# The low halves of pieces read back from device memory: a VectorE subtract in place of a ScalarE copy and an accumulating transfer

## The chip, the cores and the metric

One core of one Trainium2 chip runs the whole kernel. The metric is the device time of the kernel in microseconds; lower is better. Engines are named as the profile names them: PE is TensorE, PEld its weight loads, DVE is VectorE, ACT is ScalarE, POOL is GpSimd, SP is SyncE, which here issues nearly all DMAs.

## What is computed

One step of a hybrid encoder layer over 2048 prompt frames and 8 x 16 sample frames, 1024 channels, all in float32. The projection makes eight blocks of 1024 columns; branch a mixes positions and goes through `w_o_a`, branch b is a gated convolution of 31 taps with a layer norm and `w_o_b`; both are gated, added and go through `w_out`.

```python
h = _rmsnorm(x, norm_g) * (1 + scale) + shift
z = h @ w_in + b_in
u, v, gate_a, glu_a, glu_b, gate_b, merge_a, merge_b = jnp.split(z, SPLITS, axis=-1)
y_a = jax.nn.gelu(u) * _spatial_proj(_layernorm(jax.nn.gelu(v), ln_v_g, ln_v_b), w_spatial, b_spatial)
y_a = (y_a * jax.nn.silu(gate_a)) @ w_o_a
g_cat = jnp.concatenate([conv_hist, glu_a * jax.nn.sigmoid(glu_b)], axis=1)
dw = lax.conv_general_dilated(g_cat, conv_w[:, None, :], (1,), 'VALID', ...) + conv_b
y_b = (jax.nn.silu(_layernorm(dw, ln_c_g, ln_c_b)) * jax.nn.silu(gate_b)) @ w_o_b
m = jax.nn.sigmoid(merge_a) * y_a + jax.nn.sigmoid(merge_b) * y_b
x = x + gate * (m @ w_out)
```

## The kernel before

**Products in halves.** Matmuls take operands rounded to a shorter format (fp32r in the profile). To keep float32's digits, every operand is split in two: hi is the rounded value, lo the rest, and a product is three matmuls, hi with hi, hi with lo, lo with hi. Names end in h and l (ya4h, ya4l; wh, wl). `split` is the usual way to make the two: ScalarE copies hi (L592), VectorE subtracts lo = value - hi (L594).

**Groups and stages.** The rows are worked on in three groups of 768, 768 and 640 columns (channels lie on the 128 partitions, rows of the sequence along the columns). The stages follow each other as first_products(0), branch_a(0), first_products(1), branch_a(1), branch_b(0), first_products(2), branch_a(2), output(0), branch_b(1), branch_b(2); `prepare` makes the next group's normed input between them. What doesn't fit into on-chip memory between stages is put away: `put` (L709) stores a tile of 128 rows in device memory, under names such as away_ya, away_ma, away_dw, away_sum, and `get` (L714) reads it back into a slot (yab, mab, dwb, sumb). All such tiles lie in one pool of 47 slots, tag "u"; a tile that takes over a slot waits until the old one's readers are done, stores among them.

**What reads pieces back in halves.** `halves_of` does it for the eight tiles ya of each branch_a, and for the eight tiles ma of output(0): 32 calls. It gets the tile, copies hi on ScalarE (L722), copies lo = -hi on ScalarE (L724), and then `added` (L700) lets a DMA on GpSimd's queue add the tile from device memory onto lo. branch_a multiplies ya with `w_o_a` (`product`, L615, tiles oa) and the result with the sigmoid of merge_a (L1180, mab, put away as ma).

**First products in seven.** first_products makes a pair of column blocks with seven products instead of eight (Strassen's scheme, `strassen`, L660; ga, gb, ma, mb and so on are its outputs, bga, bgb, bma, bmb its bank B in PSUM, acga, acgb its banks A and C). On bank B products A11, S2, S3 and A22 are added up one after another; between two of them `snap` (L671, ScalarE) copies the bank out as it stands, so the next of them waits for that copy. VectorE adds bank C (L681) and banks A and C (L685). The last column blocks of a group (mb, gb) stand in TensorE's order beside the first products of branch_a.

**The convolution** is 31 taps per tile on VectorE (L951, tile dw, reading the tile gb or gsb that comes back from away_g; its first tap is ScalarE's, L936). The layer norm's statistics in branch_b start from sumb (dmh L592, dml L594) and end in sums over partitions (dv, L529).

**What sets the order.** No order is written out. `Plan` gathers all operations with a cost in us, a due time and, for transfers, a lag, and simulates five engines: an engine takes, of its operations that are ready and have a slot, the one that is due first. In that order the instructions are issued, each engine in sequence. So an operation that is added, taken away or moved to another engine changes the order of others too.

Of the kernel before, what the change touches and what calls it, by code (L numbers as in the profile page):

```python
# [9 lines left out]
F32 = mybir.dt.float32  # L10
F32R = mybir.dt.float32r
AF = mybir.ActivationFunctionType
# [72 lines left out]
class Plan:  # L85
# [22 lines left out]
    def op(self, eng, cost, fn, reads=(), writes=(), due=0.0, nb=-1, step=None, func=None,  # L108
           commute=False, lat=0.0):
        o = Op()  # L110
        o.eng, o.cost, o.fn, o.due, o.nb, o.step, o.func = eng, cost, fn, due, nb, step, func
        o.lat = lat
        o.users, o.ready, o.seq = [], 0.0, len(self.ops)
        deps = set()
        vals = set()
        for x in reads:
            p = x if isinstance(x, Part) else x.part(None)
            vals.add(p.val)
            deps.update(p.writers)
            p.readers.append(o)  # L120
        for x in writes:
            p = x if isinstance(x, Part) else x.part(None)
            vals.add(p.val)
            if commute and p.commuting and not p.readers:
                p.writers.append(o)
                continue
            deps.update(p.readers)
            deps.update(p.writers)
            p.writers, p.readers, p.commuting = [o], [], commute
        deps.discard(o)  # L130
        for d in deps:
            d.users.append(o)
        o.n_deps = len(deps)
        o.vals = list(vals)
        for v in vals:
            v.uses += 1
        self.ops.append(o)
        return o
# [102 lines left out]
def c_dve(n):  # L241
    return n / 960.0 + 0.13
# [6 lines left out]
def c_act(n, fixed=0.15):  # L249
    return n / 1200.0 + fixed  # L250
# [7 lines left out]
def encoder_kernel(ctx: ExitStack, tc: tile.TileContext, xT, hist0, cT, w_ada, w_cols, w_v,  # L258
                   vecs, convw, wsT, bsp, bv_row, lnv_rows,
                   yT, ncp, ncs, vout):  # L260
    nc = tc.nc
# [11 lines left out]
    op = plan.op  # L273
# [25 lines left out]
    def slot(name, dt=F32):  # L299
        uid[0] += 1  # L300
        return plan.val("u", [P, UW], dt, f"{name}_{uid[0]}")
# [47 lines left out]
    def new_step():  # L349
# [7 lines left out]
       reads=[vec], writes=[vec], due=-9)  # L357
    op("pool", 0.5, lambda: make_identity(nc, ident.t), writes=[ident])
    op("dve", 0.1, lambda: nc.vector.tensor_tensor(fold.t, ident.t[:, :9], ident.t[:, 9:18], op=ALU.add),
       reads=[ident], writes=[fold], due=-9)  # L360
    op("pool", 0.3, lambda: nc.gpsimd.memset(ones.t, 1.0), writes=[ones])
    op("act", 0.3, lambda: nc.scalar.activation(ones_r.t, ones.t, AF.Copy), reads=[ones], writes=[ones_r],
       due=-6)
    op("pool", 0.2, lambda: nc.gpsimd.memset(half.t, -0.5), writes=[half])
    op("act", 0.3, lambda: nc.scalar.activation(cin.t, cin.t, AF.Silu), reads=[cin], writes=[cin],
       due=-9, func="silu")
# [223 lines left out]
    def split(src, n, due, name):  # L590
        hi, lo = slot(f"{name}h", F32R), slot(f"{name}l", F32R)
        op("act", c_act(n, 0.1), lambda: nc.scalar.activation(hi.t[:, :n], src.t[:, :n], AF.Copy),  # L592
           reads=[src], writes=[hi], due=due)
        op("dve", c_dve(n), lambda: nc.vector.tensor_tensor(  # L594
            lo.t[:, :n], src.t[:, :n], hi.t[:, :n].bitcast(F32), op=ALU.subtract),
           reads=[src, hi], writes=[lo], due=due)
        return hi, lo
# [100 lines left out]
    def added(out, out_ap, src, src_ap, due):  # L698

        op("pool", C_ADD, lambda: nc.gpsimd.dma_start(out=out_ap(), in_=src_ap(), accum_op=ALU.add),  # L700
           reads=src, writes=out, due=due, lat=L_ADD)


    away = {}
# [7 lines left out]
    def get(x, j, n, due, nb):  # L712
        a, v = away[x, j], slot(f"{x[0]}b")
        op("sp", n * 512 / 340e3, lambda: nc.sync.dma_start(out=v.t[:, :n], in_=a.t[:, :n]),  # L714
           reads=[a], writes=[v], due=due, nb=nb, lat=3.5)
        return v

    def halves_of(x, j, n, due):

        v, a = get(x, j, n, due - 1, due - 2), away[x, j]  # L720
        hi, lo = slot(f"{x[0]}{j}h", F32R), slot(f"{x[0]}{j}l", F32R)
        op("act", c_act(n, 0.1), lambda: nc.scalar.activation(hi.t[:, :n], v.t[:, :n], AF.Copy),  # L722
           reads=[v], writes=[hi], due=due)
        op("act", c_act(n, 0.1), lambda: nc.scalar.activation(  # L724
            lo.t[:, :n], hi.t[:, :n].bitcast(F32), AF.Copy, scale=-1.0), reads=[hi], writes=[lo], due=due + 0.01)
        added([lo], lambda: lo.t[:, :n].bitcast(F32), [a], lambda: a.t[:, :n], due + 0.02)
        return hi, lo


    def segments(gi, b0, bn):  # L730
# [437 lines left out]
    def branch_a(gi):  # L1168

        ns, npr, p0 = GROUPS[gi]  # L1170
        n = ns + npr
        nt, nh = n // P, n // 2
        last = gi == len(GROUPS) - 1
        cuts = halves(n)
        sA = step_no[0]
        ya = [halves_of(("ya", gi), k, n, sA - 2 + k * 0.1) for k in range(KC)]
        for j in range(KC):
            ps, st = product(W_OA + j, ya, wide(n), f"oa{gi}_{j}")
            m = get(("ma", gi), j, n, st, st - 1)
            op("dve", c_dve(n), lambda m=m, b=(lambda ps=ps, m=m: banks(ps, m, n)): nc.vector.tensor_tensor(  # L1180
                b()[1], b()[0], b()[1], op=ALU.mult), reads=[ps, m],
               writes=[m], due=st + 1.5)
            put(("ma", gi), j, m, n, st + 1.6)
# [63 lines left out]
    def output(gi, ms=None):  # L1247
# [6 lines left out]
        if ms is None:  # L1254
            ms = [halves_of(("ma", gi), k, n, step_no[0] - 2 + k * 0.1) for k in range(KC)]
# [51 lines left out]
    for q in range(4):  # L1307
        due, scale_whole, shift_whole = ADA[q]
        ada("scale", q, 4 * q * D, due, scale_whole)
        ada("shift", q, (4 * q + 2) * D, due, shift_whole)  # L1310
    h = prepare(0, due=0, nb=-1, dr=DR)
# [6 lines left out]
    h = prepare(1, due=step_no[0] + PREP_DUE, nb=step_no[0] + PREP_NB)  # L1318
# [3 lines left out]
    h = prepare(2, due=step_no[0] + PREP_DUE, nb=step_no[0] + PREP_NB)  # L1322
# [67 lines left out]
```

## Time and profile before

| | us |
|---|---|
| median of 3 runs (lowest to highest) | 2112.56 (2109.44 to 2116.53) |
| profiled execution: its own time | 2110.4 |
| its span, first to last instruction | 2108.7 |
| TensorE busy | 2060.6 (98%) |
| VectorE busy | 1693.0 (80%) |
| ScalarE busy | 931.0 (44%) |
| GpSimd busy | 89.5 (4%) |

The mean granted TensorE clock over the span is 0.992 of full speed. Busy time counts instructions that run, not issue or waiting.

### The profile page before, as it was taken

The numbers are of one execution on the slowest core, as the hardware profiler recorded it, in microseconds if no ns is written. First come the engines' busy times: TensorE is split into PE (matmuls) and PEld (weight loads), VectorE is DVE, ScalarE is ACT, GpSimd is POOL, SyncE is SP. The second block draws the span as 40 slices with busy tenths as digits, with TensorE's granted clock in tenths as the row PEclk, the third lists the DMA queues.
The fourth block names the chain that finished last, engine by engine and source line by source line (L and its number), as shares of the span: only waits on it lengthen the run. The fifth ranks groups of instructions, "written<-read, shape, count | busy, mean of one in ns | idle before, by whom it ended". The sixth has DMA issues, their size and how long they took to land.

```text
span 2108.7 us, 33303 instructions
## 1 busy us (share of the span) xinstructions
PE 2060.6 (98%) x12810; PEld 1966.2 (93%) x12810; DVE 1693.0 (80%) x2407; ACT 931.0 (44%) x1356; POOL 89.5 (4%) x107
## 2 busy tenths in 40 slices
PE   7999999999999999999999999999999999999997
PEld 3999998999979999999998889999999999888997
DVE  5759988999899969688547899769999974956855
ACT  3354455455642343444446432434544544523432
POOL 0000000000100000000001010000000011010000
PEclk9999999999999999999999999999999999999998
DMA  8538777688975477887889876599989999376463
GB/s 328 205 141 295 260 298 270 225 312 294 318 252 204 137 264 247 279 262 246 285 262 324 312 218 181 174 342 335 335 300 319 335 314 342 119 232 221 154 196 118
DMA packets 190927, 540.58 MB, mean 256 GB/s; under 512 B 22064, under 2 KB 39728, under 8 KB 190768
## 3 DMA queue, kind: packets, MB, share of 16 engines
q1 hardware_dynamic: 180256, 511.11, 68.3%
q0 software_dynamic: 10512, 27.33, 7.4%
q8 instruction: 101, 1.65, 0.3%
q14 instruction: 58, 0.48, 0.1%
HBM read 375.47 MB, written 162.89 MB: 255 GB/s over the span
## 4 chain that ended last, share of the span: by engine, by line
PE 87%; DMA 6%; DVE 3%; issue 2%; ACT 0%; SPq 0%; POOL 0%; POOLq 0%; DVEq 0%; ACTq 0%
PE v L1032 9%; PE ob L615 9%; PE out L615 7%; PE bga L660 5%; PE bgla L660 5%; PE bu L660 5%; PE oa L615 4%; PE bglb L660 4%; PE bma L660 4%; PE bmb L660 4%; PE acga L660 3%; PE acu L660 3%; PE acgla L660 3%; PE acma L660 3%; PE bgb L660 3%; PE acglb L660 3%
## 5 line engine op out<-in xcount | busy, mean ns | idle before, releaser
L951 DVE SCALAR_TENSOR_TENSOR dw<-gb,cw,dw 128x768 f32<-128x768 f32 (+1 forms) x720 | 658.5, 924 | 37.8 <-ACT dw L936 32.2
L384 DVE TENSOR_TENSOR w<-ra,w 128x1024 fp32r<-128x1024 f32 x112 | 121.6, 1087 | 37.3 <-ACT w L382 36.3
L382 ACT ACTIVATE wh<-wr 128x1024 fp32r<-128x1024 f32 x88 | 91.9, 1053 | 133.7 <-PE ob L615 76.5
L382 ACT ACTIVATE w<-ra 128x1024 fp32r<-128x1024 f32 x112 | 105.6, 947 | 61.6 <-PE acgla L660 17.4
L384 DVE TENSOR_TENSOR wl<-wr,wh 128x1024 fp32r<-128x1024 f32 x88 | 106.9, 1216 | 3.3 <-ACT wh L382 3.3
L384 DVE TENSOR_TENSOR w<-rb,w 128x512 fp32r<-128x512 f32 x112 | 75.4, 685 | 40.6 <-ACT w L382 40.4
L382 ACT ACTIVATE w<-rb 128x512 fp32r<-128x512 f32 x112 | 67.9, 626 | 77.5 <-PE acglb L660 13.0
L947 DVE SCALAR_TENSOR_TENSOR dw<-gsb,cw,dw 128x128 f32<-128x128 f32 x240 | 82.5, 344 | 0.9 <-ACT dw L940 0.9
L1047 ACT ACTIVATE v<-v 128x768 f32<-128x768 f32 (+1 forms) x24 | 19.4, 810 | 110.4 <-DVE v L1043 94.4
L691 ACT ACT_TABLE_LOAD x50 | 64.2, 1283 | 0.9
L1230 DVE TENSOR_TENSOR mbb<-ob,mbb 128x768 f32<-128x768 f32 (+1 forms) x24 | 21.8, 910 | 51.0 <-PE ob L615 51.0
L671 ACT ACTIVATE u<-bu,vec 128x384 f32<-128x384 f32 (+1 forms) x48 | 26.9, 561 | 58.7 <-PE bu L660 58.6
L671 ACT ACTIVATE glb<-bglb,vec 128x384 f32<-128x384 f32 (+1 forms) x48 | 27.0, 562 | 57.4 <-PE bglb L660 57.0
L671 ACT ACTIVATE gla<-bgla,vec 128x384 f32<-128x384 f32 (+1 forms) x48 | 27.0, 563 | 51.3 <-PE bgla L660 48.0
L671 ACT ACTIVATE ga<-bga,vec 128x384 f32<-128x384 f32 (+1 forms) x48 | 26.9, 560 | 47.4 <-PE bga L660 46.7
L671 ACT ACTIVATE ma<-bma,vec 128x384 f32<-128x384 f32 (+1 forms) x48 | 27.0, 562 | 44.5 <-PE bma L660 43.0
L671 ACT ACTIVATE gb<-bgb,vec 128x384 f32<-128x384 f32 (+1 forms) x48 | 26.9, 561 | 35.9 <-PE bgb L660 33.0
L671 ACT ACTIVATE mb<-bmb,vec 128x384 f32<-128x384 f32 (+1 forms) x48 | 26.8, 559 | 32.6 <-PE bmb L660 32.1
L1277 DVE SCALAR_TENSOR_TENSOR x<-out,mod_gate,x 128x768 f32<-128x768 f32 (+1 forms) x24 | 20.1, 836 | 26.0 <-PE out L615 18.6
L1180 DVE TENSOR_TENSOR mab<-oa,mab 128x768 f32<-128x768 f32 (+1 forms) x24 | 21.7, 906 | 20.6 <-DMA mab<-away_ma__232 5.6
L382 ACT ACTIVATE w<-rs 128x1024 fp32r<-128x1024 f32 x28 | 29.6, 1056 | 16.0 <-DVE rs L445 9.2
L384 DVE TENSOR_TENSOR w<-rs,w 128x1024 fp32r<-128x1024 f32 x28 | 34.1, 1220 | 3.1 <-ACT w L382 1.1
(1068 smaller groups left out, 7190.5 us busy)
## 6 DMA issues: line engine op xcount, KB each, us to landing
w<-kept SPq DMA_DIRECT2D x224, 512.0 KB, 5.4
kept<-w SPq DMA_DIRECT2D x112, 512.0 KB, 4.0
ra<-in_w_cols SPq DMA_DIRECT2D x84, 512.0 KB, 6.6
wr<-in_w_cols SPq DMA_DIRECT2D x80, 512.0 KB, 6.2
rb<-in_w_cols SPq DMA_DIRECT2D x28, 512.0 KB, 5.9
rb<-in_w_cols SPq DMA_DIRECT2D x56, 256.0 KB, 5.3
x<-in_xT SPq DMA_DIRECT2D x32, 384.0 KB, 7.4
wa<-in_w_ada SPq DMA_DIRECT2D x24, 384.0 KB, 7.0
```

The costliest lines, as they stand in the source:

```text
L382: op("act", c_act(n, 0.1), lambda: nc.scalar.activation(hi_ap(), src_ap(), AF.Copy), reads=[src], writes=[hi], due=due)
L384: op("dve", c_dve(n), lambda: nc.vector.tensor_tensor(lo_ap(), src_ap(), hi_ap().bitcast(F32), op=ALU.subtract), reads=[src, hi], writes=[ ...
L615: nc.tensor.matmul(ps.t[:, z, :cw_], a.t[:, ks], b.t[:, c0:c0 + cw_], start=first and i == 0, stop=last and i == 2)
L660: nc.tensor.matmul(acc(), a.t[:, o + k * P:o + (k + 1) * P], b.t[:, xo:xo + nh], start=first and k == 0 and i == 0, stop=k == 3 and i == 2 ...
L671: op("act", c_act(nh, 0.28), lambda: nc.scalar.activation(half(i, z), B(), f, bias=col(bias, i)), reads=[bk, vec], writes=[out[i].part(z)] ...
L691: op("act", c_act(nh), lambda: nc.scalar.activation(half(1, 1), half(1, 1), func), reads=[out[1].part(1)], writes=[out[1].part(1)], due=st ...
L947: op("dve", c_dve(ns), lambda q=q: nc.vector.scalar_tensor_tensor(dw.t[:, :ns].rearrange("p (s l) -> p s l", l=LS), g3()[:, :, q:q + LS], ...
L951: op("dve", c_dve(npr), lambda q=q: nc.vector.scalar_tensor_tensor(dw.t[:, ns:n], g.t[:, q:q + npr], cw.t[:, j, q:q + 1], dw.t[:, ns:n], o ...
L1032: nc.tensor.matmul(o(), a.t[:, sl], view(b)[:, k % 4, :], start=state["n"] == 0, stop=state["n"] == 3 * KC - 1, skip_group_check=True)
L1180: op("dve", c_dve(n), lambda m=m, b=(lambda ps=ps, m=m: banks(ps, m, n)): nc.vector.tensor_tensor(b()[1], b()[0], b()[1], op=ALU.mult), re ...
L1230: op("dve", c_dve(n), lambda m=m, b=(lambda ps=ps, m=m: banks(ps, m, n)): nc.vector.tensor_tensor(b()[1], b()[0], b()[1], op=ALU.mult), re ...
L1277: op("dve", c_dve(bn), lambda j=j, x=x, ps=ps, bn=bn: nc.vector.scalar_tensor_tensor(x.t[:, :bn], ps.t.rearrange("p a b -> p (a b)")[:, :b ...
```

## The change

`halves_of` ends in `split` on the tile that came back. So lo is value - hi, made by VectorE from the tile on chip; the ScalarE copy lo = -hi and the accumulating DMA on GpSimd's queue are gone. Lines behind L720 move up by seven (L951 becomes L944, L936 becomes L929, L1180 becomes L1173).

```diff
--- before.py
+++ after.py
@@ -717,14 +717,7 @@
 
     def halves_of(x, j, n, due):
 
-        v, a = get(x, j, n, due - 1, due - 2), away[x, j]
-        hi, lo = slot(f"{x[0]}{j}h", F32R), slot(f"{x[0]}{j}l", F32R)
-        op("act", c_act(n, 0.1), lambda: nc.scalar.activation(hi.t[:, :n], v.t[:, :n], AF.Copy),
-           reads=[v], writes=[hi], due=due)
-        op("act", c_act(n, 0.1), lambda: nc.scalar.activation(
-            lo.t[:, :n], hi.t[:, :n].bitcast(F32), AF.Copy, scale=-1.0), reads=[hi], writes=[lo], due=due + 0.01)
-        added([lo], lambda: lo.t[:, :n].bitcast(F32), [a], lambda: a.t[:, :n], due + 0.02)
-        return hi, lo
+        return split(get(x, j, n, due - 1, due - 2), n, due, f"{x[0]}{j}")
 
 
     def segments(gi, b0, bn):
```

GpSimd's order loses the 32 DMAs and keeps all else. The other engines are ordered anew by `Plan`; three places follow. The names are the tiles with a number each.

ScalarE, the end of first_products(0) beside branch_a(0). Before, from the copy of bank bgb to the last one:

```order
L671 ACTIVATE gb_656_5357<-bgb_655_5297,vec 128x384
L722 ACTIVATE ya4h_5434<-yab_5247 128x768
L722 ACTIVATE ya5h_5436<-yab_5264 128x768
L724 ACTIVATE ya4l_5441<-ya4h_5434 128x768
L671 ACTIVATE gb_657_5451<-bgb_655_5297,vec 128x384
L724 ACTIVATE ya5l_5456<-ya5h_5436 128x768
L722 ACTIVATE ya6h_5465<-yab_5271 128x768
L722 ACTIVATE ya7h_5483<-yab_5290 128x768
L724 ACTIVATE ya6l_5487<-ya6h_5465 128x768
L724 ACTIVATE ya7l_5491<-ya7h_5483 128x768
L671 ACT_TABLE_LOAD
```

And with the change, from the copies for mb and gb to the last but one for gb:

```order
L671 ACTIVATE mb_641_5347<-bmb_639_5142,vec 128x384
L671 ACTIVATE gb_656_5351<-bgb_655_5293,vec 128x384
L592 ACTIVATE ya4h_5366<-yab_5245 128x768
L592 ACTIVATE ya5h_5370<-yab_5262 128x768
L592 ACTIVATE ya6h_5374<-yab_5267 128x768
L592 ACTIVATE ya7h_5391<-yab_5288 128x768
L671 ACTIVATE mb_641_5347<-bmb_639_5142,vec 128x384
L691 ACTIVATE mb_641_5347<-mb_641_5347 128x384
L671 ACTIVATE gb_656_5351<-bgb_655_5293,vec 128x384
L929 ACTIVATE dw_329_5436<-gb_5396,vec,cw 128x768
L671 ACTIVATE gb_657_5443<-bgb_655_5293,vec 128x384
```

The four hi copies stand together, and dw (L929), which reads the tile gb that comes back from away_g, moved ahead of a copy of bank bgb. In SP's order that get stood behind both mb stores and the get of mab; now it stands ahead of them, right behind the four kept stores.

TensorE at the same place. Before, behind the product S3 (tiles t3) on bank bgb come the first products of branch_a:

```order
L660 MATMUL bgb_655_5297<-t3h_1013,w_5316 128x384 x2
L660 MATMUL bgb_655_5297<-t3l_1017,w_5316 128x384
L660 MATMUL bgb_655_5297<-t3h_1013,w_5316 128x384
L615 MATMUL oa_0_727_5443<-ya0h_5163,wh_5354 128x512
L615 MATMUL oa_0_727_5443<-ya0h_5163,wh_5354 128x256
```

With the change the next product on the same bank (tiles t20 to t23) follows at once:

```order
L660 MATMUL bgb_655_5293<-t3h_1013,w_5285 128x384 x2
L660 MATMUL bgb_655_5293<-t3l_1017,w_5285 128x384
L660 MATMUL bgb_655_5293<-t3h_1013,w_5285 128x384
L660 MATMUL bgb_655_5293<-t20h_812,w_5306 128x384
L660 MATMUL bgb_655_5293<-t20l_838,w_5306 128x384
```

Twelve matmuls of bgb moved ahead of the first oa products; the same happens one product earlier, so that three products on bgb (t20, t3, t20) follow each other. Which products stand ahead of the last of them is the same as before but for the oa products. Behind it the oa products come in the order ya0 to ya7; before, pairs were interleaved (ya0 to ya3 of the first, then of the second, then ya4 on).

VectorE, the end of first_products(1) beside branch_a(1). Before:

```order
L951 SCALAR_TENSOR_TENSOR dw_947_10233<-gb_10198,cw,dw_947_10233 128x768
L384 TENSOR_TENSOR wl_10505<-wr_10291,wh_10485 128x1024
L951 SCALAR_TENSOR_TENSOR dw_947_10233<-gb_10198,cw,dw_947_10233 128x768 x6
L681 TENSOR_TENSOR gb_1289_10565<-acgb_1286_10430,gb_1289_10565 128x384
L951 SCALAR_TENSOR_TENSOR dw_947_10233<-gb_10198,cw,dw_947_10233 128x768
L384 TENSOR_TENSOR wl_10599<-wr_10297,wh_10594 128x1024
```

With the change:

```order
L944 SCALAR_TENSOR_TENSOR dw_947_10225<-gb_10190,cw,dw_947_10225 128x768
L594 TENSOR_TENSOR ya3l_10506<-yab_10365,ya3h_10411 128x768
L944 SCALAR_TENSOR_TENSOR dw_947_10225<-gb_10190,cw,dw_947_10225 128x768
L594 TENSOR_TENSOR ya4l_10528<-yab_10381,ya4h_10510 128x768
L594 TENSOR_TENSOR ya5l_10534<-yab_10408,ya5h_10526 128x768
L594 TENSOR_TENSOR ya6l_10545<-yab_10414,ya6h_10532 128x768
L594 TENSOR_TENSOR ya7l_10559<-yab_10432,ya7h_10536 128x768
L681 TENSOR_TENSOR gb_1289_10549<-acgb_1286_10416,gb_1289_10549 128x384
L384 TENSOR_TENSOR wl_10576<-wr_10289,wh_10551 128x1024
```

Five subtracts stand ahead of gb's L681, where taps of the convolution stood.

## Rows read from the trace of the kernel before

**Rows 1.** The page, busy time by engine (share of the span, instructions).
```profile
PE 2060.6 (98%) x12810; PEld 1966.2 (93%) x12810; DVE 1693.0 (80%) x2407; ACT 931.0 (44%) x1356; POOL 89.5 (4%) x107
```

**Rows 2.** TensorE's waits: who for whom; us in total, times, longest.
```profile
PE bgb L660 <- ACT gb L671: 8.4, 3, 4.7
PE dv L529 <- DVE dq L1206: 3.4, 1, 3.4
...
PE oa L615 <- DMA ya6l<-away_ya__152: 2.4, 1, 2.4
...
PE oa L615 <- DMA ya7l<-away_ya__153: 0.7, 1, 0.7
PE bmb L660 <- ACT mb L671: 0.7, 1, 0.7
```

**Rows 3.** Windows behind four stalls: busy us by engine, granted clock, DMA share, GB/s.
```profile
582.00:594.00 12.00, 8.96 (x34) 7.34 (x35) 7.58 (x9) 5.59 (x7) 0.00 (x0) 0.72 1.04 365
1142.00:1150.00 8.00, 6.72 (x29) 6.63 (x30) 5.32 (x6) 7.60 (x11) 2.64 (x4) 0.79 1.05 342
1702.00:1710.00 8.00, 5.97 (x30) 5.97 (x31) 2.32 (x3) 6.75 (x11) 2.61 (x3) 0.79 1.06 335
1802.00:1812.00 10.00, 8.13 (x35) 7.39 (x36) 8.11 (x12) 2.88 (x4) 1.99 (x1) 0.66 0.38 126
```

**Rows 4.** Timeline, several engines: start, us, what; in brackets idle before and releaser.
```profile
566.45 0.52 PE L615 MATMUL oa<-ya0h,wh 128*128 128x512 f32 x2
...
579.14 1.03 ACT L936 ACTIVATE dw<-gb,vec,cw 128x768 f32<-128x768 f32 x1 [5.93 <-DMA gb<-away_g__132]
...
1138.83 0.85 ACT L722 ACTIVATE ya4h<-yab 128x768 fp32r<-128x768 f32 x1 [4.72 <-DMA away_ma__249<-ma]
...
1143.28 0.44 PE L660 MATMUL bgb<-t20h,w 128*128 128x384 f32 x1 [3.50 <-ACT gb L671]
...
1700.09 0.74 ACT L722 ACTIVATE ya4h<-yab 128x640 fp32r<-128x640 f32 x1 [5.47 <-DMA away_ma__322<-ma]
...
1704.03 0.63 PE L660 MATMUL bgb<-t20h,w 128*128 128x320 f32 x1 [4.72 <-ACT gb L671]
...
1777.67 0.85 ACT L592 ACTIVATE dmh<-sumb 128x768 fp32r<-128x768 f32 x1 [12.81 <-DMA sumb<-away_sum__201]
...
1778.55 0.96 DVE L594 TENSOR_TENSOR dml<-sumb,dmh 128x768 fp32r<-128x768 f32 x1 [9.85 <-ACT dmh L592]
```

**Rows 5.** Windows over the stretches in which the pieces come back, columns as in rows 3.
```profile
540.00:590.00 50.00, 46.69 (x251) 43.40 (x250) 38.20 (x43) 31.55 (x44) 7.86 (x9) 0.95 1.04 327
1110.00:1160.00 50.00, 46.12 (x254) 44.05 (x253) 38.28 (x40) 30.44 (x42) 7.88 (x9) 0.97 1.03 323
1680.00:1730.00 50.00, 45.28 (x299) 45.03 (x298) 36.84 (x69) 28.19 (x41) 7.85 (x9) 0.97 1.01 322
1735.00:1775.00 40.00, 39.99 (x261) 38.34 (x260) 20.33 (x33) 17.50 (x21) 7.82 (x9) 1.00 1.05 314
```

**Rows 6.** DMA views, 540 to 590, then 1110:1160, 1680:1770: KB, us from issue to landing.
```profile
q1 hardware_dynamic: 4229, 12.75, 67.5%
q0 software_dynamic: 1296, 3.54, 36.6%
...
gb<-away_g__132 SPq DMA_DIRECT2D x1, 399.0 KB, 14.9
yab<-away_ya__141 SPq DMA_DIRECT2D x1, 384.0 KB, 6.4
...
away_ma__249<-ma SPq DMA_DIRECT2D x1, 384.0 KB, 14.1
...
sumb<-away_sum__201 SPq DMA_DIRECT2D x1, 384.0 KB, 11.0
...
away_ma__322<-ma SPq DMA_DIRECT2D x1, 320.0 KB, 14.4
```

**Rows 7.** The instructions of line L594: count, ns min/median/max, first and last start, shapes.
```profile
L594 DVE TENSOR_TENSOR yb0l<-gbb,yb0h x3: 814/950/950, 1200.7 to 1956.9; 128x768 fp32r<-128x768 f32 x2, 128x640 fp32r<-128x640 f32 x1
```

## The prediction

> **What bounds the kernel now.** The page's busy line says TensorE: 2060.6 of 2108.7 us [rows 1]. Nothing on another engine counts unless TensorE waits for it, so the view to read next is that of TensorE's waits, longest first [rows 2]. They are few: 8.4 us in three waits of gate products (bgb) for ScalarE's copies of their bank (gb L671, the longest 4.7 us), 3.4 us of dv L529 for VectorE, and 2.4 and 0.7 us of oa products directly for ya6l and ya7l, two of the accumulating transfers themselves.
>
> The granted clock adds to them. Each of four stalls is followed by a stretch in which the view by windows shows less than 1.00 [rows 3]; 1.00 is 2.4 GHz, and the dips are to the 1.2 GHz level. Length times (1 - clock) is what each lost: 12 x 0.28 = 3.4 us, 8 x 0.21 = 1.7, 8 x 0.21 = 1.7, 10 x 0.34 = 3.4.
>
> Call the sites 1 to 4: branch_a(0) near 582 us, branch_a(1) near 1140, branch_a(2) near 1700, and output(0) with the first statistics of branch_b(1) near 1800. The waits for ya6l and ya7l are site 1's. The timeline puts a bgb wait of 3.50 us at 1143.28 and one of 4.72 at 1704.03 [rows 4]. So the sites cost 3.1 + 3.4 = 6.5, 3.5 + 1.7 = 5.2, 4.7 + 1.7 = 6.4 and 3.4 + 3.4 = 6.8 us: **24.9 us in all, the most that the change can give back there.**
>
> Next, why they stall. ScalarE's rows just before [rows 4]: at site 2 ya4h waits 4.72 us for the landing of a store (away_ma__249; ya4h takes its source's slot), and four more copies stand ahead of the copy for which TensorE waits; at site 3 it is the same with 5.47 us. At site 4 the statistics wait 12.81 us for the get of sumb, and VectorE's chain that begins there ends at dv, late. So it is transfers that land late, and the stretches in which the pieces come back show why: the 16 DMA engines are full in all of them (share 1.01 to 1.05) [rows 5], and in the first the software queue, which carries the accumulates, takes 36.6% for 3.54 MB beside the hardware queue's 67.5% for 12.75 MB [rows 6]: 10.3 points per MB against 5.3. A get of 384 KB lands in 6.4 us at the start of that stretch, the two stores above take 14.1 and 14.4, the get of gb 14.9, that of sumb 11.0 [rows 6].
>
> **The change part by part.** Removed: 32 accumulates, 16 of 768 columns and 8 of 640 for ya, 8 of 768 for ma, with GpSimd's issues; and 32 ScalarE copies lo = -hi, each as wide as a hi copy (0.85 and 0.74 us, the two ya4h of [rows 4]), some 26 us of an engine that is 44% busy. Added: 32 VectorE subtracts. The same operation stands in the trace, L594 [rows 7]: 0.95 us for 768 columns, 0.81 for 640, together 24 x 0.95 + 8 x 0.81 = 29 us, some 7 us per stretch of [rows 5]. VectorE is idle there for 50 - 38.2 = 11.8 us at site 1, 11.7 at site 2, 13.2 at site 3, and 19.7 of 40 in the ma stretch, 9.85 us of it in one piece before dml [rows 4]. So they fit by amount, and I cost them at nothing; what covers them is that idle time, and without it they would cost the 29 us.
>
> On this the Trainium skill speaks against the change: "Perfetto Trace Analysis", section "Optimizing Scalar/DVE Operations", says that where VectorE is saturated it may make sense to move work from it to ScalarE, and this does the reverse. By that rule the sum would be a loss of up to the 29 us; the rows on the stretches leave VectorE 11 us and more, which is why I don't go by it, and it is the last rival below.
>
> What each site keeps:
>
> Site 2. The store ahead of ya4h was issued at 1138.8 - 14.1 = 1124.7. With the software queue's third of the engines gone I let such a transfer take two thirds, 9.5 us (bounds: 6.4, the fastest get of those rows, and 14.1, nothing gained). It lands near 1134; the four copies of 0.85 us end by 1139, and TensorE comes for the bank at 1143.28 - 3.50 = 1139.8. Five subtracts now stand on VectorE ahead of gb L681, which TensorE needs a product later (12 matmuls of 46.12/254 = 0.18 us [rows 5], 2.2 us); they can start with the copies, so I leave 1 us. Saved 5.2 - 1 = 4.2.
>
> Site 3. The same with 1700.1 - 14.4 = 1685.7 and 9.6 us: 1695.3, three copies of 0.74 us and a weight copy (1.1 us by its width) end at 1698.6, and TensorE comes at 1704.03 - 4.72 = 1699.3. VectorE has four subtracts ahead of gb L681 there, of 0.81 us; I leave 1.4 us. Saved 6.4 - 1.4 = 5.0.
>
> Site 4. At two thirds of 11 us sumb lands 3.7 us earlier, so that dv's 3.43 us and its dip could go. But eight subtracts (7.6 us) now stand ahead of that chain, in an idle time of 9.85 us, and the store of the last convolution piece (away_dw) stands right ahead of the gets on SP's queue, so the gets wait if VectorE makes that piece later. Between nothing and 6.8 us I take just over half: 3.8.
>
> Site 1. ya6l and ya7l no longer wait for a transfer. But the order is new: three gate products follow each other on bank bgb, with a copy of the bank between each. One such neighbourhood is in the trace, bmb waiting for mb L671, 0.7 us [rows 2]; two cost 1.4. And the copy before the last of them now stands behind dw L929 on ScalarE, which waits for the get of gb. That get landed at 579.1 (dw's start), 14.9 us after its issue at 564.2 [rows 4, 6]; it now stands four rows earlier on SP's queue, ahead of the mb stores, by which I put it near 560. At 10 us it lands at 570; dw (1.03) and the copy (half as wide as ya4h's, 0.5) end at 571.5. The products ahead of that wait are the same as before, where the first oa product follows them at 566.45 [rows 4]; so they end at 567.1 with the first neighbourhood. A stall of 4.4 us, and a dip of 1.7: lost 0.7 + 4.4 + 1.7 = 6.8 against 6.5, **saved -0.3**. The bounds: a get of 6.4 us leaves a stall of 0.8 and no dip (+5.0); one of 14.9 leaves 9.3 and 3.4 (-6.9).
>
> Sum: 4.2 + 5.0 + 3.8 - 0.3 = **12.7 us**. The profiled execution took 2110.4 us; the median of the runs, 2112.56, is 2.2 above it. So 2097.7 beside the profile, and 2100 for the median.
>
> **The rivals.** Full gain: transfers fall back to 6 or 7 us and all four sites run through: 2112.6 - 24.9 = 2088. For it: the accumulates take over a third of the engines. Against it: the two new neighbourhoods, and a hardware queue that has enough work waiting to fill what is freed.
>
> Hidden anyway: weight loads and prefetches that come earlier take the freed share, stores and gets land as late as before, and the stalls form again at the same places. Only the 2.4 + 0.7 us for ya6l and ya7l with their dip go, less the 1.4, or not even these: 2107 to 2113. For it: the stalls of sites 2 to 4 are for stores and gets, none for an accumulate, and the hardware queue alone holds two thirds. Against it: per MB the accumulates hold the engines twice as long.
>
> Slower: VectorE's order. Its rows run in sequence, and at each of sites 1 to 3 four to six subtracts stand ahead of gb L681. If one is late (its hi copy, its get, a slot that TensorE frees), all behind it is late: the last gate product then waits for five subtracts, 4.8 us, less 2.2 us of TensorE work, and 1.7 for a dip: 4.3 us per site, 13 for three. With none of the stores' lateness gone that is 2126; with none of the 29 us hidden, 2141. It decides once the subtracts start later than the bank's copy, or where the idle 11.7 us falls under the 7 us added; at site 2 the idle time that is there now is of the right size, which speaks against it.
>
> **How the numbers follow.** A gain of 6 to 20 us, as summed: 0.55, centre 2100, its own range 2093 to 2106. Full gain, 20 to 25 us: 0.15. Hidden anyway: 0.20, of which a quarter is just over 6 us faster. Slower: 0.10. The runs of before lie 0.3% (some 6.3 us) apart, about what can be told from no change. Faster by more than that: 0.55 + 0.15 + 0.05 = 0.75; within it 0.17; slower 0.08, as a little of the last rival stays within. For 8 in 10 the range leaves out some of the full gain and the slower cases: 2089 to 2113.
>
> **What would show it.** At sites 2 and 3 the store ahead of ya4h lands in about 9.5 us, no bgb wait is above 1.5 us, and the clock stays at 1.00 behind it. At site 1 bgb waits for gb, behind dw L929, for 1 to 9 us. dv's wait is under 2 us. Wrong would be: bgb waits of 3 us and more at sites 2 and 3 still, gb L681 late behind the subtracts, or TensorE waiting for VectorE's ya pieces.

## The result: 26 us faster, and the profile after

| | before | changed |
|---|---|---|
| median, us (lowest to highest) | 2113.61 (2109.44 to 2116.53) | 2087.75 (2086.67 to 2090.24) |
| ratio, 95% interval | | 0.9881 (0.9865 to 0.9897) |
| profiled execution: time, span, us | 2110.4, 2108.7 | 2086.87, 2085.2 |
| mean granted TensorE clock | 0.992 | 0.997 |

The forecast was 2100 with a range from 2089. The time lies just under the range, at the value of the rival called full gain (2088). The busy time of the engines on the page after, for [rows 1]:

```profile
PE 2050.9 (98%) x12810; PEld 1959.9 (94%) x12810; DVE 1719.8 (82%) x2439; ACT 911.9 (44%) x1326; POOL 62.1 (3%) x75
```

VectorE has 27 us more (29 were put), ScalarE 19 us less, GpSimd 27 less. TensorE has as many matmuls as before and is busy for 9.7 us less: it ran them less often at the lower clock. Its waits, for [rows 2]:

```profile
PE bgla L660 <- ACT gla L671: 4.7, 2, 4.0
...
PE bgb L660 <- ACT gb L671: 1.3, 2, 0.7
PE bmb L660 <- ACT mb L671: 0.7, 1, 0.7
```

The waits for dv, ya6l and ya7l are gone, that of bgb fell from 8.4 to 1.3 us. New is bgla with 4.7 us, of which more below. The windows at the four places of [rows 3] (the work there now comes up to 23 us sooner, so all but the first are wider), and at the new wait:

```profile
582.00:594.00 12.00, 12.00 (x71) 10.51 (x70) 11.44 (x13) 5.99 (x7) 0.00 (x0) 1.00 0.95 355
1130.00:1150.00 20.00, 20.00 (x116) 18.37 (x116) 19.26 (x22) 10.47 (x13) 0.00 (x0) 1.00 0.95 348
1690.00:1710.00 20.00, 20.00 (x139) 20.00 (x139) 17.11 (x30) 7.46 (x11) 0.00 (x0) 1.00 0.91 323
1780.00:1812.00 32.00, 32.00 (x190) 28.36 (x189) 29.08 (x35) 18.49 (x22) 1.99 (x1) 1.00 0.26 90
1344.00:1360.00 16.00, 11.95 (x77) 11.76 (x77) 9.17 (x15) 12.64 (x25) 0.93 (x1) 0.89 0.88 266
```

TensorE is busy for the whole of the four windows, at 1.00; only the fifth has a dip, 16 x 0.11 = 1.8 us. The stretches in which the ya pieces come back, for [rows 5] (the third is ten us earlier than there):

```profile
540.00:590.00 50.00, 48.66 (x277) 46.15 (x276) 48.14 (x56) 34.91 (x46) 0.88 (x1) 1.00 0.97 343
1110.00:1160.00 50.00, 50.00 (x287) 47.22 (x286) 47.55 (x51) 27.30 (x36) 0.88 (x1) 1.00 0.94 336
1670.00:1720.00 50.00, 50.00 (x344) 50.00 (x343) 46.84 (x82) 24.13 (x35) 0.87 (x1) 1.00 0.90 327
```

The DMA engines are still all but full (0.97, 0.94, 0.90), and VectorE went from 38.2 to 48.1, from 38.3 to 47.6 us of 50. The DMA views, for [rows 6]:

```profile
q1 hardware_dynamic: 5566, 16.73, 92.8%
q0 software_dynamic: 144, 0.39, 4.3%
...
gb<-away_g__132 SPq DMA_DIRECT2D x1, 399.0 KB, 5.3
...
away_ma__249<-ma SPq DMA_DIRECT2D x1, 384.0 KB, 7.1
...
sumb<-away_sum__201 SPq DMA_DIRECT2D x1, 384.0 KB, 7.3
...
away_ma__322<-ma SPq DMA_DIRECT2D x1, 320.0 KB, 6.5
```

The hardware queue took over what the software queue gave up: 16.73 MB in place of 12.75, at 92.8/16.73 = 5.5 points per MB (5.3 before). All the same the four transfers shown land sooner: gb in 5.3 us (14.9), the stores in 7.1 and 6.5 (14.1 and 14.4), sumb in 7.3 (11.0). A share near 1 (1.04 before, 0.97 now) says little about how long a transfer takes; what changed is what else stands in the engines while it runs.

### The profile page after: what moved, and what is told of

It is laid out like the page before. It is cut to its first block, busy times and chain, and to the rows that moved or that the text cites. A ratio compares the mean times of both kernels' runs of the same rounds, so it can differ in the third digit from the quotient of the medians.

```text
span 2085.2 us, 33208 instructions
## 1 busy us (share of the span) xinstructions
PE 2050.9 (98%) x12810; PEld 1959.9 (94%) x12810; DVE 1719.8 (82%) x2439; ACT 911.9 (44%) x1326; POOL 62.1 (3%) x75
## 5 line engine op out<-in xcount | busy, mean ns | idle before, releaser
L944 DVE SCALAR_TENSOR_TENSOR dw<-gb,cw,dw 128x768 f32<-128x768 f32 (+1 forms) x720 | 658.5, 923 | 23.9 <-ACT dw L929 18.7
L1040 ACT ACTIVATE v<-v 128x768 f32<-128x768 f32 (+1 forms) x24 | 19.5, 811 | 102.2 <-DVE v L1036 99.5
L671 ACT ACTIVATE u<-bu,vec 128x384 f32<-128x384 f32 (+1 forms) x48 | 27.0, 563 | 61.1 <-PE bu L660 59.4
L671 ACT ACTIVATE glb<-bglb,vec 128x384 f32<-128x384 f32 (+1 forms) x48 | 27.0, 563 | 56.3 <-PE bglb L660 55.6
L671 ACT ACTIVATE gla<-bgla,vec 128x384 f32<-128x384 f32 (+1 forms) x48 | 27.1, 564 | 52.8 <-PE bgla L660 52.7
L671 ACT ACTIVATE ga<-bga,vec 128x384 f32<-128x384 f32 (+1 forms) x48 | 27.0, 562 | 44.7 <-PE bga L660 43.8
L671 ACT ACTIVATE gb<-bgb,vec 128x384 f32<-128x384 f32 (+1 forms) x48 | 27.1, 564 | 43.8 <-PE bgb L660 43.6
L671 ACT ACTIVATE ma<-bma,vec 128x384 f32<-128x384 f32 (+1 forms) x48 | 27.0, 562 | 40.7 <-PE bma L660 40.5
L1270 DVE SCALAR_TENSOR_TENSOR x<-out,mod_gate,x 128x768 f32<-128x768 f32 (+1 forms) x24 | 20.1, 836 | 27.6 <-PE out L615 24.6
L671 ACT ACTIVATE mb<-bmb,vec 128x384 f32<-128x384 f32 (+1 forms) x48 | 26.9, 560 | 32.0 <-PE bmb L660 31.7
L1275 ACT ACTIVATE ysq<-x 128x768 f32<-128x768 f32 (+2 forms) x28 | 18.4, 658 | 40.2 <-DVE x L1270 33.2
```

The costliest lines, as they stand in the source:

```text
L671: op("act", c_act(nh, 0.28), lambda: nc.scalar.activation(half(i, z), B(), f, bias=col(bias, i)), reads=[bk, vec], writes=[out[i].part(z)] ...
L944: op("dve", c_dve(npr), lambda q=q: nc.vector.scalar_tensor_tensor(dw.t[:, ns:n], g.t[:, q:q + npr], cw.t[:, j, q:q + 1], dw.t[:, ns:n], o ...
L1040: op("act", c_act(m * VC), lambda v=v, m=m: nc.scalar.activation(v.t[:, :m * VC], v.t[:, :m * VC], AF.Gelu_apprx_tanh), reads=[v], writes=[v],
L1270: op("dve", c_dve(bn), lambda j=j, x=x, ps=ps, bn=bn: nc.vector.scalar_tensor_tensor(x.t[:, :bn], ps.t.rearrange("p a b -> p (a b)")[:, :b ...
L1275: op("act", c_act(bn), lambda x=x, sq=sq, bn=bn: nc.scalar.activation(sq.t[:, :bn], x.t[:, :bn], AF.Square), reads=[x], writes=[sq], due=s ...
```

## The experiments

Theory 1 is that of the prediction: the accumulates hold the DMA engines, and other transfers land late. Theory 2: the new order of the engines, or ScalarE's shorter row, makes the gain. Theory 3: only the waits for the accumulates themselves count. Ratios are to runs of the kernel before on the same chip.

**No transfer** (kernel before, all else in its order):

```diff
-        added([lo], lambda: lo.t[:, :n].bitcast(F32), [a], lambda: a.t[:, :n], due + 0.02)
+        op("pool", C_ADD, lambda: None, reads=[a], writes=[lo], due=due + 0.02, lat=L_ADD)
```

> The kernel before, every engine in the order of before, without the 32 accumulating transfers (the lo pieces stay -hi, so this part of the computation is left out); both ScalarE copies stay. Theory 1 (the accumulates fill the DMA engines, so that other stores and gets land late): most of the 24.9 us come back, 2087 to 2093, the stores ahead of ya4h at sites 2 and 3 land in 6 to 8 us, no bgb wait for gb above 1.5 us, no wait at dv. Theory 2 (the new order of the engines, or ScalarE's shorter row, makes the gain): little changes, 2107 to 2113. Theory 3 (only the waits for the accumulates themselves count): the 3.1 us at ya6l and ya7l and their dip of 3.4 go, 2105 to 2108.

2084.69 us, ratio 0.9869 (0.9854 to 0.9883), somewhat faster than theory 1's range. The order is that of before row by row, and no copy or subtract was moved; so theory 2 falls, and theory 3 too, whose bound was 2105. Of the waits in [rows 2] only that of bmb is left. The DMA views of the first and the second stretch:

```profile
q0 software_dynamic: 144, 0.39, 4.4%
...
gb<-away_g__132 SPq DMA_DIRECT2D x1, 399.0 KB, 4.8
...
away_ma__249<-ma SPq DMA_DIRECT2D x1, 384.0 KB, 8.5
```

The get of gb takes 4.8 us, the store ahead of site 2's ya4h 8.5. The 0.39 MB left on the software queue are one accumulate of the convolution's sums (away_sum), which goes onto device memory and stands in that stretch before and after the change too.

**Plain transfer** (the same order, bytes and queue, without adding):

```diff
-        added([lo], lambda: lo.t[:, :n].bitcast(F32), [a], lambda: a.t[:, :n], due + 0.02)
+        op("pool", C_ADD, lambda: nc.gpsimd.dma_start(out=lo.t[:, :n].bitcast(F32), in_=a.t[:, :n]),
+           reads=[a], writes=[lo], due=due + 0.02, lat=L_ADD)
```

> The kernel before, in its order, with the same 32 transfers on GpSimd's queue as plain reads of the same bytes in place of accumulates (lo then holds the piece itself, so the computation is changed in that part). Theory 1 by bytes (the bytes on the engines are what delays the others): near before, 2105 to 2113. Theory 1 by the accumulate (10.3 against 5.3 points of the engines per MB): with half of the engines' time given back, 2092 to 2102, and the software queue at 5 to 6 points per MB. Theories 2 and 3: within 3 us of before, since the order and the waits stay.

2087.68 us, ratio 0.9885 (0.9870 to 0.9900): as good as the change, with every byte still moved, and better than the range put for it (2092 to 2102). Its DMA views of the first and the second stretch (software queue: packets, MB, share; then KB and us to landing):

```profile
q0 software_dynamic: 784, 3.54, 20.1%
...
gb<-away_g__132 SPq DMA_DIRECT2D x1, 399.0 KB, 7.8
...
away_ma__249<-ma SPq DMA_DIRECT2D x1, 384.0 KB, 10.6
```

The same 3.54 MB hold the engines for 20.1% in place of 36.6, in 784 packets in place of 1296 [rows 6]. So it is not the bytes, it is the adding: 10.3 points per MB against 5.7. Both figures have the accumulate away_sum in them; without its 0.39 MB and some 4.3 points the eight pieces take 10.3 and 5.0 points per MB. The store at site 2 lands in 10.6 us, and that is early enough there; one bgb wait of 1.1 us is left, at site 3.

**Half accumulates** (before, each accumulate on half the columns):

```diff
-        added([lo], lambda: lo.t[:, :n].bitcast(F32), [a], lambda: a.t[:, :n], due + 0.02)
+        added([lo], lambda: lo.t[:, :n // 2].bitcast(F32), [a], lambda: a.t[:, :n // 2], due + 0.02)
```

> The kernel before in its order, each of the 32 accumulating transfers on half the columns (the lo pieces of the other half stay -hi: that part of the computation is left out). Theory 1a (what counts is the time for which the accumulates hold the DMA engines): half of 36.6% is what the plain reads of the same bytes took, so as those: 2086 to 2091, the software queue at 18 to 20% of the engines in the first stretch. Theory 1b (an accumulating transfer delays others or itself by its kind, whatever its bytes): it still lands in some 8 us and the stalls at ya6l, ya7l and bgb stay: 2098 to 2112.

2088.65 us, ratio 0.9891 (0.9875 to 0.9908).

```profile
q0 software_dynamic: 1296, 1.97, 22.2%
...
gb<-away_g__132 SPq DMA_DIRECT2D x1, 399.0 KB, 8.6
...
away_ma__249<-ma SPq DMA_DIRECT2D x1, 384.0 KB, 11.3
```

As many packets as the whole accumulates (1296), 22.2% of the engines (18 to 20 were put), and the time of the plain reads; of the waits one of 2.6 us for bgb and one of 1.6 for ya7l are left. Theory 1a holds, 1b falls: what counts is the time for which the engines are held. Over before, half accumulates, plain reads and none, with the software queue's share of the first stretch at 36.6, 22.2, 20.1 and 4.4%, the store at site 2 lands after 14.1, 11.3, 10.6 and 8.5 us.

**Copies kept** (both ScalarE copies, the sum on VectorE):

```diff
-        added([lo], lambda: lo.t[:, :n].bitcast(F32), [a], lambda: a.t[:, :n], due + 0.02)
+        op("dve", c_dve(n), lambda: nc.vector.tensor_tensor(
+            lo.t[:, :n], v.t[:, :n], lo.t[:, :n].bitcast(F32), op=ALU.add),
+           reads=[v, lo], writes=[lo], due=due + 0.02)
```

> The kernel before with both ScalarE copies kept, and a VectorE addition lo = lo + piece in place of the accumulating transfer: ScalarE keeps its 26 us, VectorE gets the same 29 us as with the change. Theory 1: as the changed kernel, 2086 to 2092. Theory 2 by ScalarE's shorter row: the copies stand again ahead of the copies of bank bgb, 2095 to 2108.

2086.81 us, ratio 0.9880 (0.9866 to 0.9895), as the changed kernel: ScalarE's copies, 20 us of its busy time (931.6 us on this page, 911.9 with the change), are worth nothing that shows here.

**Accumulates added back** to the changed kernel, into a tile nobody reads (the two lines that make this tile and fill it with zeros are left out here):

```diff
+        a = away[x, j]
+        op("pool", C_ADD, lambda: nc.gpsimd.dma_start(out=spare.t[:, :592], in_=a.t[:, :592], accum_op=ALU.add),
+           reads=[a], due=due, nb=due - 0.5, lat=L_ADD)
         return split(get(x, j, n, due - 1, due - 2), n, due, f"{x[0]}{j}")
```

> The changed kernel, every other engine in its order, with 32 accumulating transfers added back on GpSimd's queue, 592 of the 768 or 640 columns each, into a spare tile that nothing reads. Theory 1: three quarters of the traffic is back, and so are stalls: 2098 to 2108, with stores and gets near ya4h at 10 us and more. Theory 2 and theory 3: nothing waits for these transfers and the order is that of the change: 2087 to 2090.

2093.35 us, ratio 0.9912 (0.9896 to 0.9929): some 6 us lost, between the two ranges. That is not the test that was meant. All of them add onto the one spare tile, and by the trace each waited until the one before had landed; so they went one at a time, the first eight from 500.8 us on, and only three of these were issued in the first stretch. GpSimd's row of one of the three, and the queue in that stretch:

```profile
544.53 0.86 POOL L723 DMA_DIRECT2D spare<-away_ya__150  x1 [7.83 <-DMA spare<-away_ya__149]
```

```profile
q0 software_dynamic: 720, 1.61, 17.0%
```

17.0% in place of 36.6. Accumulates that nothing reads do cost time, more than theories 2 and 3 put (2087 to 2090), but the run is no test of the size.

**One site's pieces at a time.** `halves_of` ends in `split` for ya alone (shown), or for ma alone (the same with "ma"):

```diff
+        if x[0] == "ya":
+            return split(get(x, j, n, due - 1, due - 2), n, due, f"{x[0]}{j}")
         v, a = get(x, j, n, due - 1, due - 2), away[x, j]
```

> The change for the 24 ya pieces alone; the eight ma pieces of output(0) keep the accumulates. TensorE's order is that of the change. Theory 1: sites 1 to 3 give back their 18 us less the new stall near 1350 that the change has (some 4 us), site 4 keeps its 6.8 us: 2093 to 2097, with dv L529 waiting 2 to 4 us. If site 4's stall comes from sites 1 to 3 (it stands behind them on the engines' orders): as the changed kernel, 2087 to 2090.

> The change for the eight ma pieces alone; the ya pieces keep the accumulates, and TensorE's order is that of before. Theory 1: only site 4's 6.8 us come back, 2104 to 2108, and dv doesn't wait. If site 4 stalls for VectorE's backlog or SP's order and not for the transfers: 2110 to 2114.

ya: 2089.71 us, ratio 0.9898 (0.9882 to 0.9915), in the range put for a site 4 that hangs on sites 1 to 3; ma: 2105.88, ratio 0.9976 (0.9967 to 0.9986). TensorE's waits with ya alone, then with ma alone:

```profile
PE dv L529 <- DVE dq L1208: 1.0, 1, 1.0
```

```profile
PE bgb L660 <- ACT gb L671: 7.1, 2, 3.7
...
PE oa L615 <- DMA ya6l<-away_ya__152: 2.3, 1, 2.3
```

ma alone gives back 5.9 us of medians and no dv wait is left, as site 4's cost said (6.8), while the bgb waits stay at 7.1 us. With ya alone dv waits 1.0 us in place of the 2 to 4 expected, and the dip behind it is 1.7 us in place of 3.4 (15 us from 1785 on at a clock of 0.89), though the ma accumulates are all there and sumb takes 9.6 us. So some 4 of site 4's 6.8 us go with ya's part too, and the two gains don't add: 22.1 and 5.9 us of medians against 25.9 for both. dv's row in the two traces, before and with ya alone:

```profile
1803.87 2.72 PE L529 MATMUL dv<-ones,dq 128*128 128x1 f32 x12 [3.43 <-DVE dq L1206]
```

```profile
1782.80 1.50 PE L529 MATMUL dv<-ones,dq 128*128 128x1 f32 x12 [1.02 <-DVE dq L1208]
```

Counted back from where TensorE comes to dv (1800.44 and 1781.78), the get of sumb, issued at 1766.68 and at 1746.89, leaves 1.1 us sooner and takes 1.4 us less, which is what the wait lost. Why it leaves sooner wasn't tried apart.

**Subtracts twice** (the changed kernel in its order; then only those of odd tiles). In place of the subtract of `split`, with the lines that get the piece and copy hi left out:

```diff
+        def twice():
+            for _ in range(2):          # second run: range(1 + j % 2)
+                nc.vector.tensor_tensor(
+                    lo.t[:, :n], src.t[:, :n], hi.t[:, :n].bitcast(F32), op=ALU.subtract)
+        op("dve", c_dve(n), twice, reads=[src, hi], writes=[lo], due=due)
```

> The changed kernel in its order, with every one of the 32 subtracts issued twice (same result), 29 us more on VectorE, as much as the change added. Rival A (VectorE's room is used up: 48 of 50 us busy in the first stretch): TensorE waits for gb L681 and for the ya pieces, 2096 to 2115. Rival B (taps of the convolution move into later idle time, and only order matters): 2087 to 2092.

> The changed kernel in its order, with every second of the 32 subtracts issued twice: half of the 29 us that cost the whole gain when all were doubled. By room (gb L681 ends 1.5, 1.1 and 1.5 us before TensorE needs it in the changed kernel; three, three and two further subtracts of 0.87, 0.87 and 0.74 us come ahead of it): waits of some 1.1, 1.5 and 0 us, no dips, 2089 to 2093. By amount (each us added on VectorE costs 0.9, as it did over the whole doubling): 2098 to 2103.

All twice: 2113.59 us, ratio 1.0006 (0.9996 to 1.0016), the whole gain lost. Every second: 2091.13, ratio 0.9900 (0.9883 to 0.9917), 3 to 4 us lost. TensorE's waits for VectorE, all twice and then every second:

```profile
PE acgb L660 <- DVE gb L681: 12.5, 3, 4.7
```

```profile
PE acgb L660 <- DVE gb L681: 2.5, 2, 1.6
```

This is the prediction's last rival, at its place: gb L681 behind the subtracts, one wait per site. It has no price below the room and then costs in full, with a dip behind a long wait: of the 26 us that all twice lost, 12.5 are these waits, 2.0 a wait of dv, and some 12 the lower clock (mean 0.991, 0.997 with the change). The room in the changed kernel is read from VectorE's row and TensorE's next at site 1:

```profile
570.21 0.56 DVE L681 TENSOR_TENSOR gb<-acgb,gb 128x384 f32<-128x384 f32 x1 [0.29 <-ACT gb L671]
```

```profile
572.44 0.34 PE L660 MATMUL acgb<-h4h,w 128*128 128x384 f32 x1
```

gb L681 ends at 570.77, TensorE comes to the product that needs it at 572.44: 1.7 us to spare. The same rows give 2.4 and 2.1 us at sites 2 and 3, more than the expectation put (1.5, 1.1, 1.5). Ahead of gb L681 stand all eight, eight and seven subtracts, counted from ya0, so doubling them costs 8 x 0.87 - 1.7 = 5.3, 8 x 0.87 - 2.4 = 4.6 and 7 x 0.74 - 2.1 = 3.1 us; the three waits are 4.7, 4.4 and 3.4. Every second: four, four and three of them, 1.8, 1.1 and 0.1; measured 1.6, 0.9 and none.

**Subtracts on GpSimd**, planned at twice VectorE's cost (against the lines of `split`):

```diff
-        op("dve", c_dve(n), lambda: nc.vector.tensor_tensor(
+        op("pool", 2 * c_dve(n), lambda: nc.gpsimd.tensor_tensor(
             lo.t[:, :n], src.t[:, :n], hi.t[:, :n].bitcast(F32), op=ALU.subtract),
```

> The changed kernel with the 32 subtracts on GpSimd in place of VectorE, ordered anew. No run so far shows the duration of such a subtract on GpSimd. If it takes under 2 us and leaves VectorE alone: no transfer and no VectorE work, as the run without the transfers, 2083 to 2088. If it is slower than the pace at which oa needs the pieces (8 pieces within some 25 us), TensorE waits for ya l pieces: 2092 to 2110.

2111.56 us, ratio 0.9995 (0.9984 to 1.0006). One of GpSimd's subtracts and VectorE's taps in 540 to 590 (count, busy, mean ns, idle), and three of the taps that ran beside such subtracts:

```profile
L724 POOL TENSOR_TENSOR ya3l<-yab,ya3h 128x768 fp32r<-128x768 f32 x1 | 2.6, 2569 | 0.0
```

```profile
L951 DVE SCALAR_TENSOR_TENSOR dw<-gb,cw,dw 128x768 f32<-128x768 f32 x25 | 33.8, 1382 | 0.0
```

```profile
562.51 7.50 DVE L951 SCALAR_TENSOR_TENSOR dw<-gb,cw,dw 128x768 f32<-128x768 f32 x3
```

The subtracts of that stretch that run back to back take 2.3 to 2.7 us each, and while they run VectorE's taps slow from 1.01 us to 2.5 (1382 ns on average here). TensorE waits 10.7 us for mb L681 at site 1; so the time is just above the range of the slow case, but the wait is for VectorE, not for the pieces. The Trainium skill, "SBUF — State Buffer", section "Who interferes with whom", has a VectorE instruction with two inputs in SBUF contend with a GpSimd instruction that reads there; the taps have two, and this trace agrees.

**The new bgla wait.** In the third group the scalings of v (L1074) stand ahead of the copy of bank bgla on ScalarE. First they were made due later, then barred from early steps of the plan (both runs in one diff):

```diff
-                       writes=[v.part(i)], due=dst_ + 0.5 + c)
+                       writes=[v.part(i)], due=dst_ + 0.5 + c + (3 if gi == 2 and c else 0))      # scales_later
+                       writes=[v.part(i)], due=dst_ + 0.5 + c, nb=int(dst_) + 2 * c if gi == 2 and c else -1)  # scales_gated
```

> The changed kernel with one due time moved: in the third group the scaling of the v tiles after the first chunk (L1074) is due three steps later, so that the copy of bank bgla stands ahead of twelve of them on ScalarE. TensorE's order is that of the change. If the stall of 4.05 us near 1350 and its dip of 1.8 us are what the new order cost: 2081 to 2084. If the stall only moves (the s products then wait for the scalings): 2086 to 2089.

> The changed kernel; in the third group the scalings of the v tiles (L1074) of chunk c may not be issued before a step of the plan that is two further on for each chunk, so that at most five of them stand together, and the copies of bank bgla stand between. TensorE's order is that of the change. If the run of scalings ahead of these copies is what makes the stall near 1350 and its dip (5.9 us with the neighbour): no bgla wait above 1.5 us, 2081 to 2084. If the stall moves again: 2086 to 2089.

2086.43 us, ratio 0.9875 (0.9860 to 0.9889), and 2088.28, ratio 0.9887 (0.9870 to 0.9903): neither is apart from the change, and both keep a bgla wait (4.1 and 3.8 us). In the first it only moved: the copy that had waited went early, and a later one of the same bank stood behind eight scalings and then 1.37 us behind a store (out_vout). The timeline of ScalarE in the second, and of GpSimd:

```profile
1355.17 0.53 ACT L671 ACTIVATE gla<-bgla,vec 128x320 f32<-128x320 f32 x1 [3.12 <-DMA away_sum__201<-dw]
```

```profile
1349.52 0.93 POOL L700 DMA_DIRECT2D away_sum__201<-dw  x1 [7.03 <-DVE dw L944]
```

The scalings are out of the way, and ScalarE waits all the same, 3.12 us, for away_sum__201: an accumulate of the convolution's sums, issued at 1349.52, 5.6 us to landing. By the program's waits the copy writes into the slot that held that transfer's source, tile dw. In the changed kernel the same transfer is issued at 1348.25 and lands at 1353.3, and the copy follows at 1354.16. So the scalings mostly filled the wait. In the run without the transfer, in the order of before, this place keeps its 1.3 and 1.1 us of waits, so the loss came with the new order. That another slot would take these 4 us away is argued from this, not shown.

## Why the prediction was wrong

That the accumulates hold the DMA engines and make other transfers land late was right, and the first three experiments show it. The step that failed is the time that a transfer still takes without them, which put a stall at site 1 that never formed. All four terms of the sum were too small, those of sites 2 to 4 by what was held back for VectorE's subtracts, and one cost was missed.

- **How fast a transfer lands.** It was let take two thirds of its time. Only sumb did (7.3 of 11.0). The others took about half or less: 7.1 of 14.1, 6.5 of 14.4, 5.3 of 14.9. The step took the software queue's third off the time; the transfers that had taken longest lost more than a third.
- **Site 1**, put at -0.3, gave 5.2. The get of gb was issued at 560.04, as estimated (560), but landed 5.3 us later in place of 10, before ScalarE came to dw; so of the 6.8 us only the two neighbourhoods were left (0.67 us each):

```profile
567.02 1.02 ACT L929 ACTIVATE dw<-gb,vec,cw 128x768 f32<-128x768 f32 x1
569.60 0.58 ACT L671 ACTIVATE gb<-bgb,vec 128x384 f32<-128x384 f32 x1 [1.55 <-PE bgb L660]
```

  No wait stands at dw (567.02); the copy behind it waits for TensorE. The lower bound of the price (+5.0, a get of 6.4 us) was the truth. This is the term that failed by most, 5.5 us.
- **Sites 2 and 3**, put at 4.2 and 5.0, gave all of 5.2 and 6.4: the 1.0 and 1.4 us left over for VectorE's subtracts weren't needed, since gb L681 had 2.4 and 2.1 us to spare.
- **Site 4**, put at 3.8, gave all of 6.8: sumb landed as put, and dv has no wait. What was held back for the eight subtracts ahead of that chain wasn't needed: VectorE still sat idle for 4.11 us before dml (9.85 before).
- **The new wait near 1350** was missed: 4.05 + 0.68 us and 1.8 for the dip, against 1.3 + 1.1 us of waits at that place before (TensorE's view before: gla L671 and gla L681), 4.1 us lost.

The four sites together: 5.2 + 5.2 + 6.4 + 6.8 = 23.6, less 4.1, is 19.5 of the 23.5 us by which the span fell. Some 2 more are in short waits that went too (0.38 at 1154.9, 0.95 for kept weights near 755, 0.43 at 612, 0.3 at the start); the last 2 us I can't place, and runs of one kernel lie that far apart.

The other steps: no bgb wait above 1.5 us and the clock at 1.00 at sites 2 and 3, and dv without a wait, came as written. Full gain, given 0.15, was the case that held, and by its reason: the transfers fell back to 5.3 to 7.3 us. The neighbourhoods and the full hardware queue that spoke against it are both there, at 1.3 us and without harm. That the time falls on its 2088 so closely is luck: the 1.3 us and the 4.1 near 1350 were not in it, nor the 4 us of short waits and of unknown place that make up for most of them. "Hidden anyway" had its premise come true (the hardware queue filled the engines again) and its conclusion not. The rule of the Trainium skill that was weighed ("Perfetto Trace Analysis", "Optimizing Scalar/DVE Operations") gave no loss here; with the VectorE work once more as large it would have, as the doubled subtracts show.

## What to carry to other kernels

Where transfers land late, count for how long each kind holds the DMA engines, not its bytes: the accumulating reads cost twice a plain read of the same tile, and halving that time was worth most of what taking them away was (24.6 and 23.2 of 27.6 us). A busy share near 1 after such a change doesn't mean that nothing was gained: look at the time to landing of those transfers for which something waits. And work moved to an engine with idle time is free up to the room in front of its next urgent row, here 1.7 to 2.4 us per site, and costs in full beyond it, with a dip of the clock on top where the wait is long; read that room before adding more.

## What the runs showed of the hardware

- An accumulating read of 384 KB from device memory onto a tile goes in 144 packets and holds the 16 engines for some 10.3 points of a 50 us stretch per MB; as a plain read on the same queue it goes in 80 packets and takes some 5.0, about the hardware queue's 5.3 to 5.5. (In the first stretch stand eight such reads and the accumulate away_sum with 144 packets, 0.39 MB and 4.3%: (1296 - 144) / 8 and (784 - 144) / 8 packets, (36.6 - 4.3) / 3.15 and (20.1 - 4.3) / 3.15 points.)
- The taps, VectorE instructions with two input tiles, take 2.5 us in place of 1.01 while GpSimd subtracts tiles of the same width.
